# A two-layer hybrid block on one core: six convolution groups whose accumulators lie in PSUM alone, a norm without GpSimd, and 64-wide scores with 128 rows in both products

## The chip, the cores and the metric

The kernel runs on one core of a Trainium2 chip. The core has a tensor engine (PE, with its weight load PEld), a vector engine (DVE), a scalar engine (ACT), GpSimd (POOL) and a queue engine that only starts transfers here (SP). The metric is the device time of one execution in microseconds (us), the median of several runs. Before the change it is 2774.14 us, the median of three runs between 2769.54 and 2776.2.

## The reference, cut to what matters

Three blocks follow each other on 512 tokens of width 1024. Block A is a gated causal convolution and a cross-attention to 256 memory rows; block B an attention whose keys are picked by an index score; block C an attention with 64-wide heads beside a gated linear recurrence, then a layer of 16384 experts of which each token takes 16 for each of 8 heads. What the change touches is this:

```python
# block A: 1536 channels, 31 taps, then a norm over the channels, SiLU and a gate
h = a * jax.nn.sigmoid(gl)
h = depthwise_conv(h, conv_w) + conv_b          # each channel with its own 31 weights
y_mix = silu(layer_norm(h, g, b))
y = jnp.concatenate([y_mix, y_mem], axis=-1) * jax.nn.silu(gate)
x = layer_norm(ALPHA * x + y @ w_out, pg, pb)

# block B: index score with 8 heads of width 64, top 128 of up to 512 keys
iscore = relu(einsum('bqhd,bsd->bqhs', q_idx, k_idx))

# block C: grouped attention, 8 query heads and 2 key heads of width 64
s = einsum('bqkgd,bskd->bkgqs', qblk, k) * scale
```

## The kernel before

Activations lie transposed: 128 channels on the partitions, 512 tokens along the row, so the convolution's 1536 channels are 12 tiles `h0` to `h11`. Full precision on PE comes from splitting each operand into a high part (`hi`, `h`) and a rest (`lo`, `l`) and adding three products (`mm3`, L162 to L164). The high part of a weight tile is made on ACT (L156, `whi`), the rest on POOL or DVE (L157, `wlo`), with four buffers each.

A scheduler reads the program, simulates it on a timeline and writes one order for each engine. On the chip each engine runs its list in that order; a row that has to wait holds up all that stand behind it in its list.

Block A (`layer_a`) goes as follows. PE projects the 24 tiles of the convolution's input, then the memory keys and values (`mem_kv`), the memory queries and their attention (`mem_attn`), 16 gate tiles, and the keys and values of block B's memory attention (again `mem_kv`, with the tiles `bk` and `bv`). Beside that, DVE does the convolution: each tap is one instruction over 128x512, `acc = h[t:t+512] * weight + acc` (L599 for the first tap, L601 for the other 30). Tile 2 goes by ACT (product, L587) and POOL (sum, L590), the other eleven by DVE in the groups `CGR`, whose members take turns tap by tap. An accumulator (`cacc`) lies in one of two PSUM banks (tag `cv`); the third member of the one group with three, tile 9, has its accumulator in SBUF (tag `cva`). The last tap writes the result over `h`.

Then the sums over channels come: ACT squares (L259), POOL adds up tiles (L266, L269), PE adds over partitions with a column of ones (L289, tile `cst`), POOL makes the inverse root (L232 to L238), and PE spreads mean and inverse root over all partitions (L837, `Mb`, `Rb`, both in PSUM). In the norm DVE subtracts `Mb` (L606, 12 times); the product with the inverse root is on DVE for tiles 0, 3, 6 and 9 (L613, from PSUM) and on POOL for the other eight (L615, from `Rs`, a copy in SBUF). ACT scales, shifts and takes a tanh (L617, L619), DVE finishes SiLU (L620) and the gate (L622, whose operand comes back from memory by DMA), and the result is split in `yNh` (ACT, L182) and `yNl` (L185; DVE for even, POOL for odd tiles). PE then multiplies by `a_w_out` (tile `out`); it takes the memory part (`y12` to `y15`) first, then `y0` to `y3`, and `y4` to `y11` with a second set of weight tiles.

For 64-wide heads the split lays both parts in one tile: `split64` gives for each of two heads a tile with the high part in one half of the partitions and the rest in the other, and `twin64` gives the key's high part twice and its rest twice, once in each half. `mm64` adds two products, the first over 128 rows (L213), the second over the 64 rows that hold the query's high part (L214). It is called 24 times in block B (tile `isc`, widths 512, 384 and 256) and 32 times in block C (tile `as`, width 512).

Of the kernel before, what the change touches and what calls it, by code (L numbers as in the profile page):

```python
# [16 lines left out]
OP = mybir.AluOpType  # L17
# [28 lines left out]
MLO = 6  # L46
CGR = (0, 1), (3, 4), (5, 6), (7, 8, 9), (10, 11)
NWARM = 8
# [8 lines left out]
class Body:  # L57
# [152 lines left out]
    def mm64(self, ps, q, k, n, start=True, stop=True):  # L210

        r = slice(64 * n, 64 * n + 64)
        self.nc.tensor.matmul(ps, q, k[0], start=start, stop=False)  # L213
        self.nc.tensor.matmul(ps, q[r], k[1][r], start=False, stop=stop)  # L214

# [92 lines left out]
    def run(self):  # L308
        nc = self.nc
# [10 lines left out]
        if True:  # L320
            with self.phase("A", cva=1, slot=12, pcv=4, scr=2, asc=2, app=2, sq=2, accq=1, accs=1, back=4):
                with self.tc.tile_pool(name="mem", bufs=1) as self.mem:
                    self.layer_a()
            if self.stop == "a":
                self.right.close()
                return
            self.banks(mm=(0, 1), s=(2, 5), pt=(3, 4), o=(6, 7))
            with self.phase("B", slot=14, scr=4, asc=2, app=2, logit=3, alibi=2):
                self.layer_b()
# [206 lines left out]
    def layer_a(self):  # L536
        nc = self.nc
# [21 lines left out]
        Y = {}  # L559
        for h in range(4):  # L560
            f = self.scr("qm", tag="back")
            nc.scalar.copy(f, self.proj(W, 24 + h, self.X))
            o = self.mem_attn(self.split(f, f"qm{h}", lo="g"), kv, h)
            f = self.scr("mo")
            nc.scalar.mul(f, o, 0.5)
            nc.sync.dma_start(od[h], f)
        for j in GATES:
            if j == BKV:
                self.bkv = self.mem_kv(self.i["b_w_mkv"], "b", self.bk, "bkv", 8)
            ps = self.proj(W, 28 + j, self.X)  # L570
# [21 lines left out]
        for js in CGR:  # L592
            accs = [self.scr("cacc", tag="cva") if u == 2 else self.bank("cv", "cacc") for u in range(len(js))]
            for t in range(CK):
# [10 lines left out]
        for c in cs:  # L605
            nc.vector.tensor_tensor(c, c, Mb, op=OP.subtract)  # L606
        Rs = self.scr("Rs", tag="accs")
        nc.scalar.copy(Rs, Rb)
        for j in range(12):
            c = cs[j]  # L610
            n = self.scr("cn", tag=("asc", "app")[j % 2])
            if j % 3 == 0:
                nc.vector.tensor_tensor(n, c, Rb, op=OP.mult)  # L613
            else:
                nc.gpsimd.tensor_tensor(n, c, Rs, op=OP.mult)  # L615
            c = n
# [5 lines left out]
            nc.vector.scalar_tensor_tensor(y, c, 0.25, y, op0=OP.mult, op1=OP.mult)  # L622
            Y[4 + j] = self.split(y, f"y{j}", hi="s", lo="vg"[j % 2], x=2 <= j < 10, tag="slot" if j < 2 else "pcv")
        self.new_x()
# [826 lines left out]
```

## Time and profile before

| | before |
|---|---|
| runs | 2774.14 us (2769.54 to 2776.2) |
| profiled execution, device time | 2769.45 us |
| its span, first to last instruction | 2767.6 us |
| PE busy | 2658.0 us (96%) |
| DVE busy | 2138.1 us (77%) |
| ACT busy | 1235.6 us (45%) |
| POOL busy | 973.6 us (35%) |
| mean granted clock of PE | 0.981 |

The times below count from the start of the span. "Busy" is the time in which an engine had an instruction in work. Matmuls are pipelined: one of 128x512 is shown with 0.39 us, yet the next starts 0.23 us later, so for PE the distance from start to start tells what one costs. The granted clock is a share of 2.4 GHz; there are two levels, 2.4 and 1.2 GHz, and a number between them is a mean over a stretch.

### The profile page before, as it was taken

Reading aid. Unit: us, or ns where it says so; the run is one execution under the profiler, and the core shown is the slowest. Engines: PE = TensorE matmul, PEld = TensorE weight load, DVE = VectorE, ACT = ScalarE, POOL = GpSimd, SP = SyncE. Lnnn points to the kernel's source line nnn. Section 1 sums busy time; section 2 is a strip of 40 time slices with the busy share of each in tenths; the row PEclk is TensorE's granted clock in tenths of the full one; section 3 lists DMA queues with packets and bytes.
Section 4 is the critical chain, followed back from the end, with each engine's and each line's share of the span. In section 5 each row is a group of like instructions: output and inputs, shape, how many; then the busy total and the mean of one; then the engine's idle time right before and its main releaser. Section 6 shows DMA issues by size and latency. Waiting matters only on the chain.

```text
span 2767.6 us, 39611 instructions
## 1 busy us (share of the span) xinstructions
PE 2658.0 (96%) x14197; PEld 2316.9 (84%) x14197; DVE 2138.1 (77%) x4185; ACT 1235.6 (45%) x2155; POOL 973.6 (35%) x702
## 2 busy tenths in 40 slices
PE   9989999999999999999999898999999999999998
PEld 7878879688889877778899897999977888888887
DVE  8999875685566767754679999999677777887855
ACT  4536555455545344443424354546433333433433
POOL 5956654223224745454341522221111111211101
PEclk9999999999999999999999999999999999999999
DMA  5233455232255211136534667688988998999853
GB/s 180 92 107 118 134 170 166 61 100 81 88 184 182 92 57 51 57 107 195 174 98 138 223 224 267 233 300 309 367 305 306 323 320 308 336 353 338 317 166 99
DMA packets 205014, 534.71 MB, mean 193 GB/s; under 512 B 17681, under 2 KB 100497, under 8 KB 186897
## 3 DMA queue, kind: packets, MB, share of 16 engines
q1 hardware_dynamic: 176544, 387.83, 42.5%
q0 software_dynamic: 18432, 134.23, 12.9%
q10 hardware_dynamic: 9840, 10.12, 1.2%
q8 instruction: 112, 1.84, 0.3%
q14 instruction: 86, 0.70, 0.1%
HBM read 465.26 MB, written 66.85 MB: 192 GB/s over the span
## 4 chain that ended last, share of the span: by engine, by line
PE 50%; DVE 13%; DMA 9%; issue 4%; ACT 2%; POOL 1%; SPq 0%; DVEq 0%; POOLq 0%; ACTq 0%
PE mm L163 9%; PE mm L164 9%; PE mm L162 9%; DMA grow<-peer_uv,pidx 4%; PE po L162 3%; DMA vraw<-peer_uv 3%; PE po L163 3%; PE po L164 3%; DMA as<-a_spill 3%; DVE wlo L157 2%; DVE oh L1177 2%; PE out L162 2%; PE out L163 1%; PE out L164 1%; PE gp L1181 1%
## 5 line engine op out<-in xcount | busy, mean ns | idle before, releaser
L156 ACT CAST whi<-wraw 128x1024 fp32r<-128x1024 f32 x360 | 377.3, 1049 | 460.5 <-PE mm L163 242.6
L157 POOL TENSOR_TENSOR wlo<-wraw,whi 128x1024 fp32r<-128x1024 f32 x157 | 380.6, 2427 | 428.7 <-ACT whi L156 382.7
L1206 POOL DMA_INDIRECT grow<-peer_uv,pidx x128 | 173.8, 1358 | 748.6 <-DVE pacc L1216 711.2
L157 DVE TENSOR_TENSOR wlo<-wraw,whi 128x1024 fp32r<-128x1024 f32 x203 | 271.8, 1346 | 58.9 <-ACT whi L156 52.6
L163 PE MATMUL po<-vlo,wh 128*128 128x512 f32 x768 | 302.4, 394 | 0.3 <-DVE vlo L157 0.2
L164 PE MATMUL po<-vhi,wl 128*128 128x512 f32 x768 | 300.4, 393 | 0.0
L601 DVE SCALAR_TENSOR_TENSOR cacc<-h,vecs,cacc 128x512 f32<-128x512 f32 x319 | 235.0, 799 | 0.4
L162 PE MATMUL po<-vhi,wh 128*128 128x512 f32 x768 | 210.4, 399 | 18.4 <-ACT vhi L156 18.4
L1209 DVE SCALAR_TENSOR_TENSOR grow<-grow,hrow 128x1024 f32<-128x1024 f32 x128 | 159.0, 1242 | 54.6 <-DMA grow<-peer_uv,pidx 54.5
L157 DVE TENSOR_TENSOR vlo<-vraw,vhi 128x1024 fp32r<-128x1024 f32 x128 | 156.4, 1222 | 43.5 <-ACT vhi L156 43.2
L162 PEld LDWEIGHTS po<-vhi,wh 128*128 128x128 f32 x768 | 143.7, 189 | 47.7 <-ACT vhi L156 22.1
L1216 DVE SCALAR_TENSOR_TENSOR pacc<-grow,pwc,pacc 128x1024 f32<-128x1024 f32 x127 | 168.3, 1325 | 8.4 <-ACT pwc L1212 7.2
L163 PEld LDWEIGHTS po<-vlo,wh 128*128 128x128 f32 x768 | 144.9, 189 | 32.9 <-DVE vlo L157 2.3
L156 ACT CAST vhi<-vraw 128x1024 fp32r<-128x1024 f32 x128 | 133.8, 1046 | 82.7 <-DMA vraw<-peer_uv 78.7
L164 PEld LDWEIGHTS po<-vhi,wl 128*128 128x128 f32 x768 | 145.0, 189 | 29.4
L1211 ACT ACTIVATE pwc<-pac 128x1 f32<-128x1 f32 x128 | 26.1, 204 | 258.5 <-DVE grow L1209 258.3
L1182 ACT COPY stage<-gp 128x512 f32<-128x512 f32 x96 | 103.4, 1096 | 53.8 <-PE gp L1181 53.5
L162 PE MATMUL mm<-X0h,whi 128*128 128x512 f32 (+2 forms) x294 | 108.6, 374 | 13.9 <-ACT pa L1198 13.0
L164 PE MATMUL mm<-X0h,wlo 128*128 128x512 f32 (+2 forms) x294 | 107.2, 365 | 9.7 <-DVE wlo L157 9.6
L1181 PE MATMUL gp<-oh,oh 128*128 128x128 f32 x768 | 104.3, 282 | 11.2 <-DVE oh L1177 11.0
L1177 DVE TENSOR_SCALAR oh<-iota,rTs 128x128 f32<-128x128 f32 x384 | 113.8, 363 | 0.0
L1181 PEld LDWEIGHTS gp<-oh,oh 128*128 128x128 f32 x768 | 99.5, 194 | 15.4 <-issue 8.2
(975 smaller groups left out, 7828.2 us busy)
## 6 DMA issues: line engine op xcount, KB each, us to landing
wraw<-peer_uT SPq DMA_DIRECT2D x128, 512.0 KB, 5.7
vraw<-peer_uv SPq DMA_DIRECT2D x128, 512.0 KB, 6.5
gates<-stage SPq DMA_DIRECT2D x12, 2048.0 KB, 7.8
G<-gates SPq DMA_DIRECT2D x32, 768.0 KB, 9.5
wraw<-a_w_in SPq DMA_DIRECT2D x43, 512.0 KB, 3.6
wraw<-c_w_in SPq DMA_DIRECT2D x42, 512.0 KB, 3.6
wraw<-b_w_in SPq DMA_DIRECT2D x39, 512.0 KB, 3.5
a_spill<-pa SPq DMA_DIRECT2D x84, 192.0 KB, 4.5
```

The costliest lines, as they stand in the source:

```text
L156: nc.scalar.copy(h, src)
L157: (nc.gpsimd if lo == "g" else nc.vector).tensor_tensor(l, src, h, op=OP.subtract)
L162: nc.tensor.matmul(ps, w[0], x[0], start=start, stop=False)
L163: nc.tensor.matmul(ps, w[0], x[1], start=False, stop=False)
L164: nc.tensor.matmul(ps, w[1], x[0], start=False, stop=stop)
L601: nc.vector.scalar_tensor_tensor(a if t < CK - 1 else cs[j], src, wc, a, op0=OP.mult, op1=OP.add)
L1177: nc.vector.tensor_scalar(oh1[:, u], rows, tr[:, 0, t0 + u:t0 + u + 1], tr[:, 2, t0 + u:t0 + u + 1], op0=OP.is_equal, op1=OP.mult)
L1181: nc.tensor.matmul(ps[:, u * 128:(u + 1) * 128], oh2[:, u], oh1[:, u], start=True, stop=True)
L1182: nc.scalar.copy(stage[:, :, q4 * 4:q4 * 4 + 4].rearrange("p n t -> p t n"), ps.rearrange("p (t n) -> p t n", t=4))
L1206: nc.gpsimd.indirect_dma_start(out=gt, out_offset=None, in_=self.i["peer_uv"], in_offset=bass.IndirectOffsetOnAxis(ap=self.idx[:, n:n + 1] ...
L1209: nc.vector.scalar_tensor_tensor(gt[:, :D], gt[:, :D], 1.0, self.hrow, op0=OP.mult, op1=OP.mult, accum_out=ac)
L1216: nc.vector.scalar_tensor_tensor(self.acc, gt[:, D:], wc, self.acc, op0=OP.mult, op1=OP.add)
```

## The change

The two groups (7, 8, 9) and (10, 11) become (7, 8), (9, 10) and (11,). All accumulators of the groups take the two PSUM banks, and the SBUF buffer `cva` is gone. In the norm all twelve products with the inverse root are on DVE from PSUM, so POOL's eight and ACT's copy `Rs` go, and all twelve `yNl` are on DVE, six of them from POOL. In `mm64` the second product takes all 128 rows of query and key like the first, so that it also adds the product of both rests.

```diff
-CGR = (0, 1), (3, 4), (5, 6), (7, 8, 9), (10, 11)
+CGR = (0, 1), (3, 4), (5, 6), (7, 8), (9, 10), (11,)
...
     def mm64(self, ps, q, k, n, start=True, stop=True):
-        r = slice(64 * n, 64 * n + 64)
         self.nc.tensor.matmul(ps, q, k[0], start=start, stop=False)
-        self.nc.tensor.matmul(ps, q[r], k[1][r], start=False, stop=stop)
+        self.nc.tensor.matmul(ps, q, k[1], start=False, stop=stop)
...
-            with self.phase("A", cva=1, slot=12, pcv=4, scr=2, asc=2, app=2, sq=2, accq=1, accs=1, back=4):
+            with self.phase("A", slot=12, pcv=4, scr=2, asc=2, app=2, sq=2, accq=1, accs=1, back=4):
...
-            accs = [self.scr("cacc", tag="cva") if u == 2 else self.bank("cv", "cacc") for u in range(len(js))]
+            accs = [self.bank("cv", "cacc") for _ in js]
...
-        Rs = self.scr("Rs", tag="accs")
-        nc.scalar.copy(Rs, Rb)
...
-            if j % 3 == 0:
-                nc.vector.tensor_tensor(n, c, Rb, op=OP.mult)
-            else:
-                nc.gpsimd.tensor_tensor(n, c, Rs, op=OP.mult)
+            nc.vector.tensor_tensor(n, c, Rb, op=OP.mult)
...
-            Y[4 + j] = self.split(y, f"y{j}", hi="s", lo="vg"[j % 2], x=2 <= j < 10, tag="slot" if j < 2 else "pcv")
+            Y[4 + j] = self.split(y, f"y{j}", hi="s", lo="v", x=2 <= j < 10, tag="slot" if j < 2 else "pcv")
```

The new lists differ in block A, in a few places of block B and in the expert layer; in the attention of block C the order is the same. Lines after the edited ones have numbers that are smaller by 1, by 6 after the norm.

The first place is DVE's list in the convolution, where tile 6 starts. Before, three accumulators take turns, of which `cacc_3000` (tile 9) is the one in SBUF:

```order
L599 TENSOR_SCALAR cacc_2923<-h6_721,vecs_70 128x512
L601 SCALAR_TENSOR_TENSOR cacc_3000<-h9_922,vecs_70,cacc_3000 128x512
L601 SCALAR_TENSOR_TENSOR cacc_2922<-h5_654,vecs_70,cacc_2922 128x512
L601 SCALAR_TENSOR_TENSOR cacc_2923<-h6_721,vecs_70,cacc_2923 128x512
L601 SCALAR_TENSOR_TENSOR cacc_3000<-h9_922,vecs_70,cacc_3000 128x512
```

With the change, at the same place:

```order
L598 TENSOR_SCALAR cacc_2923<-h6_721,vecs_70 128x512
L600 SCALAR_TENSOR_TENSOR cacc_2922<-h5_654,vecs_70,cacc_2922 128x512
L600 SCALAR_TENSOR_TENSOR cacc_2923<-h6_721,vecs_70,cacc_2923 128x512
L600 SCALAR_TENSOR_TENSOR cacc_2922<-h5_654,vecs_70,cacc_2922 128x512
L600 SCALAR_TENSOR_TENSOR cacc_2923<-h6_721,vecs_70,cacc_2923 128x512
```

The tile with the SBUF accumulator has moved out of the middle to the end, as a member of the pair (9, 10) in PSUM, and tile 11 runs its last 20 taps without a partner, where it ran its last 12 so before.

The second place is POOL's list from the inverse root (`rs_o`) of the convolution's norm on. Before:

```order
L238 TENSOR_TENSOR rs_o<-rs_u,rs_r 128x4
L615 TENSOR_TENSOR cn<-h_280,Rs 128x512
L615 TENSOR_TENSOR cn<-h_347,Rs 128x512
L575 TENSOR_TENSOR g<-th,g 128x512
L578 TENSOR_TENSOR g<-g,ob 128x512
L185 TENSOR_TENSOR y14l<-g,y14h 128x512
L575 TENSOR_TENSOR g<-th,g 128x512
L578 TENSOR_TENSOR g<-g,ob 128x512
L575 TENSOR_TENSOR g<-th,g 128x512
L185 TENSOR_TENSOR y15l<-g,y15h 128x512
L615 TENSOR_TENSOR cn<-h_481,Rs 128x512
L615 TENSOR_TENSOR cn<-h_654,Rs 128x512
```

With the change:

```order
L237 TENSOR_TENSOR rs_o<-rs_u,rs_r 128x4
L574 TENSOR_TENSOR g<-th,g 128x512
L577 TENSOR_TENSOR g<-g,ob 128x512
L185 TENSOR_TENSOR y14l<-g,y14h 128x512
L574 TENSOR_TENSOR g<-th,g 128x512
L577 TENSOR_TENSOR g<-g,ob 128x512
L574 TENSOR_TENSOR g<-th,g 128x512
L185 TENSOR_TENSOR y15l<-g,y15h 128x512
L268 TENSOR_TENSOR accs<-ar_3646,ar_3652 128x512
```

The products `cn` and, further down, the odd `yNl` are gone from POOL; the gate tiles 14, 11 and 15 stay, and next comes work of the output projection.

The third place is PE's list between the convolution's sums (`cst`) and the spread inverse root (`Rb`). Before, from the spread mean (`Mb`) to `Rb`:

```order
L837 MATMUL Mb<-ident,st 128x128 x4
L163 MATMUL mm<-memx_571,whi 128x256
L164 MATMUL mm<-memx_571,wlo 128x256
L162 MATMUL mm<-memx_579,whi 128x256
L163 MATMUL mm<-memx_579,whi 128x256
L164 MATMUL mm<-memx_579,wlo 128x256
L837 MATMUL Rb<-ident,rs_o 128x128 x4
```

With the change:

```order
L831 MATMUL Mb<-ident,st 128x128 x4
L162 MATMUL mm<-X3h,whi 128x512
L163 MATMUL mm<-X3l,whi 128x512
L164 MATMUL mm<-X3h,wlo 128x512
L162 MATMUL mm<-X4h,whi 128x512
L163 MATMUL mm<-X4l,whi 128x512
L831 MATMUL Rb<-ident,rs_o 128x128 x4
```

PE has got further in its own work when it comes to the sums: 13 products of 256 columns that stood behind `cst` stand ahead of it, and it is in the next projection (512 columns) when it comes to `Rb`.

## Rows read from the trace of the kernel before

**Rows 1.** The page's first part: busy time of each engine.
```profile
PE 2658.0 (96%) x14197; PEld 2316.9 (84%) x14197; DVE 2138.1 (77%) x4185; ACT 1235.6 (45%) x2155; POOL 973.6 (35%) x702
```
**Rows 2.** Stretches: length, busy PE, PEld, DVE, ACT, POOL, PE clock, DMA share, GB/s.
```profile
100.00:200.00 100.00, 91.00 (x481) 79.22 (x480) 100.00 (x127) 39.63 (x59) 77.11 (x43) 0.95 0.34 105
```
**Rows 3.** Stretches, instructions of L601 alone: length, DVE busy, PE clock, DMA.
```profile
24.00:127.00 103.00, 86.13 (x128) 1.00 0.32 97
127.00:215.00 88.00, 78.10 (x89) 0.94 0.33 102
```
**Rows 4.** Timeline of DVE: start, duration, engine, line, tiles, count.
```profile
141.48 16.46 DVE L601 SCALAR_TENSOR_TENSOR cacc<-h,vecs,cacc 128x512 f32<-128x512 f32 x15
...
303.47 2.33 DVE L601 SCALAR_TENSOR_TENSOR cacc<-h,vecs,cacc 128x512 f32<-128x512 f32 x3
```
**Rows 5.** PE's waits, 20 to 312 us: total, times, longest.
```profile
PE mm L162 <- ACT mk L413: 5.2, 1, 5.2
PE mvt L422 <- DVE av L222: 2.1, 1, 2.1
PE mvt L422 <- ACT mvT L419: 1.7, 1, 1.7
PE msc L162 <- ACT mp L445: 1.7, 1, 1.7
```
**Rows 6.** Timeline of ACT; in brackets the wait and what ended it.
```profile
160.92 0.37 ACT L413 COPY mk<-mm 128x256 f32<-128x256 f32 x1 [6.66 <-DVE ak L222]
```
**Rows 7.** Stretches as in rows 2, memory keys and values.
```profile
160.00:170.00 10.00, 8.65 (x55) 8.65 (x56) 10.00 (x15) 4.53 (x8) 4.71 (x2) 0.70 0.19 54
...
180.00:190.00 10.00, 10.00 (x40) 8.08 (x40) 10.00 (x16) 3.32 (x6) 2.89 (x2) 0.84 0.25 91
```
**Rows 8.** Timeline of PE where the convolution ends.
```profile
316.64 0.58 PE L289 MATMUL cst<-ones,h 128*128 128x1 f32 x2 [3.51 <-DVE h L601]
```
**Rows 9.** Stretches as in rows 2, convolution's sums.
```profile
310.00:320.00 10.00, 6.49 (x43) 6.28 (x41) 6.85 (x7) 3.54 (x6) 4.71 (x3) 0.81 0.56 204
320.00:330.00 10.00, 10.00 (x62) 9.96 (x62) 2.93 (x7) 1.17 (x3) 3.10 (x9) 0.67 0.22 79
```
**Rows 10.** Groups of instructions, 0 to 700 us: busy, mean ns, idle before.
```profile
L620 DVE SCALAR_TENSOR_TENSOR cn<-th,cn 128x512 f32<-128x512 f32 x12 | 15.0, 1279 | 1.6 <-ACT th L619 1.6
...
L622 DVE SCALAR_TENSOR_TENSOR gb<-cn,gb 128x512 f32<-128x512 f32 x12 | 12.6, 1066 | 3.3 <-DMA gb<-a_gates 3.2
...
L615 POOL TENSOR_TENSOR cn<-h,Rs 128x512 f32<-128x512 f32 x8 | 10.3, 1291 | 14.7 <-DVE gb L622 6.6 <-issue 4.4 <-ACT Rs L608 3.7
```
**Rows 11.** Timeline of DVE, the subtraction of the mean.
```profile
328.09 7.27 DVE L606 TENSOR_TENSOR h<-h,Mb 128x512 f32<-128x512 f32 x12 [3.07 <-PE Mb L837]
```
**Rows 12.** Stretches as in rows 2, output projection of block A.
```profile
360.00:370.00 10.00, 8.86 (x39) 6.82 (x37) 9.91 (x12) 7.90 (x13) 5.97 (x5) 1.00 0.46 130
370.00:380.00 10.00, 5.27 (x11) 3.25 (x12) 9.97 (x10) 8.03 (x12) 5.53 (x4) 0.54 0.29 68
```
**Rows 13.** Timeline of PE where the second set of weights begins.
```profile
371.15 0.80 PE L162 MATMUL out<-y4h,whi 128*128 128x512 f32 x1 [2.29 <-ACT whi L156]
```
**Rows 14.** Timeline of PE, products of the 64-wide scores.
```profile
493.10 0.40 PE L213 MATMUL isc<-kih,qi 128*128 128x512 f32 x1
493.34 0.40 PE L163 MATMUL mm<-X1l,whi 128*128 128x512 f32 x1
...
972.14 0.49 PE L214 MATMUL as<-k0l,rq 64*128 64x512 f32 x1
972.57 0.50 PE L213 MATMUL as<-k0h,rq 128*128 128x512 f32 x1
973.00 0.49 PE L214 MATMUL as<-k0l,rq 64*128 64x512 f32 x1
```
**Rows 15.** Stretches as in rows 2, both places of the 64-wide scores.
```profile
490.00:545.00 55.00, 52.95 (x196) 36.26 (x195) 36.89 (x71) 20.59 (x37) 13.86 (x7) 0.94 0.19 58
960.00:1240.00 280.00, 266.87 (x1376) 208.21 (x1375) 200.45 (x389) 114.32 (x219) 142.74 (x132) 1.00 0.21 66
```
**Rows 16.** PE's waits, 1260 to 2768 us, the largest.
```profile
PE po L162 <- ACT vhi L156: 18.4, 10, 3.4
```

## The prediction

> **What bounds the kernel now.** I read the page first: PE is busy for 96% of the span, DVE for 77% [rows 1]. A gain therefore has to show on PE, as less work or as less waiting, and a part of the change that only frees DVE or POOL is worth what PE stood still for. The stretches then say where that is. In block A's middle DVE has not a moment's rest, 100.00 of 100 us, while PE has gaps, 91.00 of 100 [rows 2]: there DVE sets the pace. PE's list of waits names them: one of 5.2 us for a copy on ACT, and three of 2.1, 1.7 and 1.7 us, 10.7 us together [rows 5]. ACT's timeline shows that the copy of the long one had itself stood for 6.66 us behind a split on DVE [rows 6]. Where the convolution ends PE waits again, 3.51 us for the last tap [rows 8], and in the output projection it stands for the second set of weights [rows 13]. The two places of the 64-wide scores look different: PE is busy for 52.95 of 55 and 266.87 of 280 us [rows 15], so there the work of PE counts itself, and waiting is 2 and 13 us.
>
> **The convolution.** Eleven tiles of 31 taps, 341 instructions, are the same before and after. What changes is how long one takes. Between 24 and 127 us, with both accumulators in PSUM, 128 of them keep DVE for 86.13 us, 0.673 each; between 127 and 215 us, while tile 9 with its accumulator in SBUF takes turns with the others, 89 keep it for 78.10, or 0.878 [rows 3]. The worst piece is 15 in 16.46 us [rows 4]. POOL is at work for 77% of this time [rows 2], and what differs is that tile 9's taps read two operands from SBUF. The difference is 89 x 0.205 = 18.2 us of DVE, and I expect all of it to go.
>
> The Trainium skill says the same of two-operand work (SBUF — State Buffer, Who interferes with whom): a DVE instruction with two inputs in SBUF contends with a GpSimd instruction that reads SBUF, one with at most one such input does not. The trace agrees with 0.878 against 0.673 us.
>
> For PE this is worth the waits that came from a late DVE: up to 10.7 us, and the slower clock behind them. The granted clock is 0.70 and 0.84 of 2.4 GHz in two stretches of 10 us behind the waits [rows 7], a mix with the 1.2 GHz level that costs 10 x 0.30 + 10 x 0.16 = 4.6 us. That makes 15.3 at most. The 15 taps ahead of the first split took 16.46 us [rows 4] and would take 10.1 at the undisturbed pace, so DVE gets there over 6 us earlier and the longest wait should go whole; one of the short ones may stay. I take **13**, between 5 (the longest wait alone) and 15.3.
>
> **The end of the convolution.** PE gains 13, DVE 18.2 us, so the last tap comes some 5 us earlier as PE sees it. Against that, tile 11 runs 20 taps alone instead of 12, and alone a tap follows the last after 2.33 / 3 = 0.78 us [rows 4] instead of 0.67, so 8 x 0.11 = 0.9 us are lost. PE also has 13 products of 256 columns more in front of its sums. The wait of 3.51 us [rows 8] should vanish but for some tenths; it cannot turn into much more than that, because rows of DVE in front of the last taps (the splits of `bk` and two `wlo`) wait for PE themselves. What is left is the clock: 0.81 and 0.67 in the two stretches around the sums [rows 9], 1.9 + 3.3 = 5.2 us. If the wait made PE slow, it goes too; if the sums themselves do it, 24 products of one column, it stays. I take half of it and the wait: **6**, between 0 and 8.7. The third group adds no wait of its own: the accumulator of tile 11 takes the bank of tile 9, whose last reader stands ahead on the same engine.
>
> **The norm.** DVE gets 8 products and 6 rests more, 14 instructions. Undisturbed, twelve subtractions take 7.27 us, 0.606 each [rows 11], so that is 8.5 us. POOL's eight products, 1.29 us each, go, and with them the disturbance that they and the six rests cause: SiLU and gate take 1.279 and 1.066 us in the mean for the same shape [rows 10], 12 x 0.67 + 12 x 0.46 = 13.6 us above the undisturbed pace. I take a third of that to come from POOL's gate tiles, which stay, so some 9 us come back: DVE comes out even. The chain gets shorter, since POOL waited 6.6 us for DVE in five places [rows 10], and those are hops that no longer exist. On PE, the output projection lost 1.14 + 4.73 us of idle time and, at 0.54, 4.6 us of clock [rows 12], 10.5 in all, to weights that ACT could only cast after it had done `y6h` [rows 13]. In the new lists all four casts stand behind `y6h` again, and PE arrives with three us more of its work done. So most of this stall stays: I take **3**, between -8.5 (the 14 instructions uncovered) and 10.5.
>
> **The 64-wide scores.** A product of 128 rows and 512 columns lets the next one start 0.24 us later (493.10 to 493.34). Into and out of one with 64 rows it is 0.43 us on either side (972.14, 972.57, 973.00) [rows 14]. PE's weight load does not run ahead across that border. With all rows in both products there is no border: 2 x 0.20 = 0.40 us for each of the 32 in block C, 12.8 us; in block B some of the 24 are narrower and one side is less, which I put at 0.35, 8.4 us. That is 21.2 us of PE, at places where PE is busy for 95 to 96% [rows 15]. Not all of it arrives: between the products stand softmax and index sums, and DVE is at 72% in block C. A quarter lost to such waits leaves **16**, between 4 and 21.2.
>
> Here a rule of the Trainium skill speaks against the edit (TensorEngine Tiling (Array Packing), Key Properties): tiles that take half of the rows work independently and can run in parallel, so giving them up could cost. The same list says that a change of tiling mode drains the engine, which is what the 0.43 us look like; the 64-row products here stand alone between 128-row ones, and nothing runs beside them. By the first rule alone this term would be zero or a loss, by the second it is the 21 us.
>
> **Sum.** 13 + 6 + 3 + 16 = 38 us from the profiled execution's 2769.45 us: 2731 us. That execution is the lowest of those shown, 4.7 us under their median, and a median of the changed kernel may lie that much higher, so I predict **2732**.
>
> **Rivals.**
> Time that comes back as waiting. DVE is already full in block A, and in blocks B and C what PE saves it could stand idle for the next softmax. For it speaks that short waits are there already, 13 us in block C [rows 15]; against it, that they are much smaller than PE's work. It gives half of each large term and little of the small ones, 8 + 2 + 0 + 8 = 18: 2751 us.
> The border isn't what costs. If 0.43 us belong to these products for another reason than the row count, `mm64` does not do what it is meant to and its term is 0: 38 - 16 = 22, 2747 us. Against it stands that the same first product (L213) has a successor after 0.24 us where that is a 128-row one.
> Slower than before. The expert layer's lists have moved too, though its code hasn't. There PE waits 18.4 us in ten places, up to 3.4 us each, for casts that wait for the expert's rows from memory [rows 16]. If a transfer comes late in the new order, each such wait is 3.4 us; from eleven more on, all 38 us are gone, and with fifteen the time is 2782 us. Nothing says that the new order is worse there, and the ten of before may as well get fewer.
>
> **How the numbers follow.** The forecast has 0.66, with a range of its own from 2715 to 2745; the returned waiting 0.18; the border 0.11; slower through the expert layer 0.04; 0.01 is left. The range from 2714 to 2755 takes in the forecast and both middle cases but not the last, and its low end is where nearly all bounds are reached (15 + 9 + 8 + 21 = 53 would be 2716). Differences under 0.3%, 8.3 us, cannot be told from none in this kernel. Faster by more than that is 0.93 (the three cases that gain, less what a weaker sum leaves), the same 0.04, slower 0.03.
>
> **What will show it.** Right: taps at 0.67 to 0.69 us from 127 to 215 us; no wait of PE for `mk` near 156 us; `cst` reached without a wait of 3.5 us and some 15 us earlier; SiLU and gate near 0.7 us where POOL is still; products of L212 and L213 0.23 us apart. Wrong: the same idle time of PE at other rows of block A, PE standing longer before `y4`, or in block C a PE that is busy for far less than 95% while the stage is as long as before.

## The result and the profile after

| | before | after |
|---|---|---|
| runs | 2775.17 us (2769.54 to 2785.57, 4 runs) | 2736.78 us (2735.62 to 2744.85, 4 runs) |
| ratio, 95% interval | | 0.9877 (0.9857 to 0.9897) |
| profiled execution | 2769.45 us | 2735.62 us |
| mean granted clock of PE | 0.981 | 0.984 |

The change makes the kernel 38 us faster in the medians (29 to 40 by the interval) and 34 us between the two profiled executions; 2732 was forecast. The page's first part, against [rows 1]:

```profile
PE 2635.2 (96%) x14197; PEld 2315.2 (85%) x14197; DVE 2115.8 (77%) x4199; ACT 1233.8 (45%) x2154; POOL 951.0 (35%) x688
```

PE has the same 14197 products and is busy for 22.8 us less, so two thirds of those 34 us are PE's own pace (borders, clock), and one third is waiting that went. DVE has 14 instructions more and is busy for 22.3 us less.

**The convolution.** The stretch of [rows 2], and the taps alone in stretches like those of [rows 3] (they stand in L600 now; columns as there):

```profile
100.00:200.00 100.00, 100.00 (x544) 87.02 (x543) 98.45 (x152) 45.92 (x76) 83.06 (x47) 1.00 0.39 118
...
24.00:127.00 103.00, 84.66 (x126) 0.98 0.31 96
127.00:200.00 73.00, 61.14 (x92) 1.00 0.40 121
```

DVE is nearly as full as before, but it does 152 instructions in these 100 us, where it did 127; a tap takes 61.14 / 92 = 0.665 us where it took 0.878 in the mean. PE has no gap left and runs at 1.00. Its waits from 20 to 312 us, all of them, against [rows 5]:

```profile
PE memT L398 <- ACT memf L401: 3.6, 1, 3.6
PE cst L288 <- DVE h L600: 0.7, 1, 0.7
PE mm L164 <- POOL wlo L157: 0.5, 1, 0.5
```

The waits for `mk`, `mvt` and `msc` are gone. (The first row belongs to the transposes of the memory rows, from 64 to 86 us; before, it was 1.6 us, and in a second trace of the changed kernel it is 1.6 us again.)

**Where the convolution ends.** PE's timeline, against [rows 8], and the stretches around it, against [rows 9]:

```profile
303.03 0.38 PE L288 MATMUL cst<-ones,h 128*128 128x1 f32 x2 [0.71 <-DVE h L600]
...
304.89 3.55 PE L288 MATMUL cst<-ones,sq 128*128 128x1 f32 x16
```

```profile
300.00:310.00 10.00, 9.29 (x58) 9.08 (x57) 4.22 (x8) 2.48 (x5) 4.77 (x6) 0.72 0.50 154
310.00:320.00 10.00, 10.00 (x56) 8.80 (x55) 6.95 (x11) 3.05 (x5) 1.46 (x5) 0.94 0.26 79
```

PE arrives at 302.3 instead of 313.1 us and waits 0.71 instead of 3.51. The clock still falls here.

**The norm and the output projection.** Groups of instructions from 303 to 400 us (columns as in [rows 10]), and the stretches in which `y4` comes, against [rows 12]:

```profile
L614 DVE SCALAR_TENSOR_TENSOR cn<-th,cn 128x512 f32<-128x512 f32 x12 | 9.5, 798 | 1.1 <-ACT th L613 1.1
L616 DVE SCALAR_TENSOR_TENSOR gb<-cn,gb 128x512 f32<-128x512 f32 x12 | 8.2, 688 | 6.6 <-DMA gb<-a_gates 6.5
```

```profile
350.00:360.00 10.00, 8.81 (x36) 6.19 (x35) 10.00 (x14) 8.50 (x12) 0.00 (x0) 1.00 0.54 164
360.00:370.00 10.00, 10.00 (x46) 8.23 (x45) 6.31 (x11) 2.40 (x4) 0.00 (x0) 1.00 0.64 188
```

SiLU and gate take 0.80 and 0.69 us each where they took 1.28 and 1.07. POOL is idle for 20 us, PE loses 1.2 us of them, and the clock stays at 1.00; before, PE lost 5.9 us in such 20 and the clock was at 0.54 in one half. One wait on DVE is longer, 6.5 us for the gate's operand from memory against 3.2 [rows 10]; PE waits 1.1 us in all in the output projection, for weights.

**The 64-wide scores.** PE's timeline, against [rows 14]:

```profile
945.76 0.50 PE L212 MATMUL as<-k0h,rq 128*128 128x512 f32 x1 [0.52 <-DVE rq L195]
946.10 0.40 PE L213 MATMUL as<-k0l,rq 128*128 128x512 f32 x1
946.34 0.39 PE L212 MATMUL as<-k0h,rq 128*128 128x512 f32 x1
946.57 0.40 PE L213 MATMUL as<-k0l,rq 128*128 128x512 f32 x1
946.80 1.05 PE L886 MATMUL hl<-hQ,kc 128*128 128x128 f32 x8
```

Two calls take 946.80 - 945.76 = 1.04 us. The steps are 0.23 us, but the first one behind a wait is 0.34. The rows of the weight load (PEld) show what the border does: before, the weights of a product were loaded only when that product itself started (first row, of the kernel before); now they are loaded when its predecessor starts (second row, the weights of the product of 946.34).

```profile
972.57 0.19 PEld L213 LDWEIGHTS as<-k0h,rq 128*128 128x128 f32 x1 [0.24 <-issue]
```

```profile
946.10 0.19 PEld L212 LDWEIGHTS as<-k0h,rq 128*128 128x128 f32 x1
```

The whole stage of block C's scores, from the first to the last, has the same 1292 products in the same order before and after. Here it is before, after, and in the second trace of the changed kernel (columns as in [rows 2]):

```profile
971.71:1234.20 262.49, 249.85 (x1292) 194.30 (x1292) 187.12 (x368) 105.94 (x205) 132.48 (x124) 1.00 0.21 65
```

```profile
945.76:1198.80 253.04, 239.51 (x1292) 195.40 (x1293) 186.60 (x368) 105.69 (x205) 133.29 (x124) 1.00 0.22 67
```

```profile
941.60:1197.80 256.20, 243.28 (x1291) 198.75 (x1292) 186.80 (x368) 105.73 (x205) 133.41 (x124) 0.98 0.21 66
```

PE has 10.3 us less work, and 9.5 of them arrive; its idle time grows from 12.6 to 13.5 us. The second trace is 3.2 us longer because the granted clock fell there (0.98 over the stage); neither trace of the kernel before has that.

**The account by stages.** Starts read from the traces, in us. Each of the two kernels has two traces; the second ones are from the last experiments.

| start of | before | after | gain so far |
|---|---|---|---|
| first sum of the convolution's last tile | 316.6, 314.6 | 303.0, 301.7 | 13.3 |
| first score of block B (`isc`) | 493.1, 492.0 | 470.9, 468.4 | 22.9 |
| last score of block B | 542.4, 541.4 | 515.9, 511.9 | 28.0 |
| first score of block C (`as`) | 971.7, 970.6 | 945.8, 941.6 | 27.5 |
| last score of block C | 1234.2, 1233.1 | 1198.8, 1197.8 | 35.4 |
| first product of the expert layer (`po`) | 1971.3, 1971.8 | 1937.2, 1935.9 | 35.0 |
| end of the span | 2767.6, 2768.9 | 2733.8, 2729.9 | 36.4 |

The gain is made in block A and at the two places of the scores; between them and behind them the stages are as long as before, within 1.4 us in the mean.

### The profile page after: what moved, and what is told of

It reads as the page before. It is cut to its first block, busy times and chain, and to the rows that moved or that the text cites. A ratio compares the mean times of both kernels' runs of the same rounds, so it can differ in the third digit from the quotient of the medians.

```text
span 2733.8 us, 39603 instructions
## 1 busy us (share of the span) xinstructions
PE 2635.2 (96%) x14197; PEld 2315.2 (85%) x14197; DVE 2115.8 (77%) x4199; ACT 1233.8 (45%) x2154; POOL 951.0 (35%) x688
## 4 chain that ended last, share of the span: by engine, by line
PE 51%; DVE 15%; DMA 10%; issue 5%; ACT 2%; POOL 1%; SPq 0%; DVEq 0%; POOLq 0%; ACTq 0%
PE mm L162 9%; PE mm L164 9%; PE mm L163 9%; DMA grow<-peer_uv,pidx 6%; PE po L163 3%; PE po L164 3%; PE po L162 3%; DMA vraw<-peer_uv 3%; DVE wlo L157 2%; DVE oh L1171 2%; PE out L162 2%; PE out L163 2%; PE out L164 2%; PE gp L1175 1%; DVE pacc L1210 1%
## 5 line engine op out<-in xcount | busy, mean ns | idle before, releaser
L600 DVE SCALAR_TENSOR_TENSOR cacc<-h,vecs,cacc 128x512 f32<-128x512 f32 x319 | 218.0, 749 | 0.6
L1175 PEld LDWEIGHTS gp<-oh,oh 128*128 128x128 f32 x768 | 98.8, 193 | 17.2 <-issue 8.8
```

The source lines that it names most:

```text
L600: nc.vector.scalar_tensor_tensor(a if t < CK - 1 else cs[j], src, wc, a, op0=OP.mult, op1=OP.add)
L1175: nc.tensor.matmul(ps[:, u * 128:(u + 1) * 128], oh2[:, u], oh1[:, u], start=True, stop=True)
```

## The experiments

The first four put parts of the change alone, or all but one. Each ratio is against runs of the kernel before that were timed beside it (medians of 2775.24, 2775.0 and 2769.44 us).

**The convolution alone** (before, with the new groups, both kinds of accumulator in PSUM).

```diff
-CGR = (0, 1), (3, 4), (5, 6), (7, 8, 9), (10, 11)
+CGR = (0, 1), (3, 4), (5, 6), (7, 8), (9, 10), (11,)
...
-            accs = [self.scr("cacc", tag="cva") if u == 2 else self.bank("cv", "cacc") for u in range(len(js))]
+            accs = [self.bank("cv", "cacc") for _ in js]
```

> The kernel before with the six groups and all accumulators in PSUM, nothing else. Theory (tile 9's SBUF accumulator was slowed by GpSimd, and a late DVE made PE wait): taps fall to 0.67-0.69 us each everywhere, PE's waits for the memory keys go, PE reaches the convolution's sums 12 us earlier, and the time falls by 12 to 16 us, to about 2760. Rival (DVE had slack, the gain comes from the norm): DVE is early, but PE waits the same time for the norm's results, and the time falls by less than 5 us.

Measured: 2756.83 us (6 runs), ratio 0.9934 (0.9913 to 0.9956), so 12 to 24 us faster. The first sum of the last tile comes at 299.7 us, 16 us earlier, and block B's scores begin at 473.1, 19 us earlier. It is the largest part of the change.

**The norm alone** (before, with the products on DVE and no POOL in the splits).

```diff
-        Rs = self.scr("Rs", tag="accs")
-        nc.scalar.copy(Rs, Rb)
...
-            if j % 3 == 0:
-                nc.vector.tensor_tensor(n, c, Rb, op=OP.mult)
-            else:
-                nc.gpsimd.tensor_tensor(n, c, Rs, op=OP.mult)
+            nc.vector.tensor_tensor(n, c, Rb, op=OP.mult)
...
-            Y[4 + j] = self.split(y, f"y{j}", hi="s", lo="vg"[j % 2], ...
+            Y[4 + j] = self.split(y, f"y{j}", hi="s", lo="v", ...
```

> The kernel before with the norm's twelve products and twelve rests on DVE alone, nothing else. Theory (DVE comes out even, the hops through GpSimd go): the stall of PE ahead of y4 shrinks from 10 us to some 5, time down by 3 to 9 us, about 2768. Rival (14 more instructions on the busiest engine): time up by 3 to 8 us, about 2780.

Measured: 2782.54 us (12 runs), ratio 1.0021 (1.0006 to 1.0036), 2 to 10 us slower. My theory missed this, and the rival's size came, but not at the rival's place. That place got faster: from the first sum to block B's scores it is 170.8 us, before 176.5 and 177.4. PE's waits in the output projection, from 325 to 395 us, first in this kernel, then with the convolution alone, which has the old norm:

```profile
PE out L164 <- DVE wlo L157: 0.9, 1, 0.9
PE out L162 <- ACT whi L156: 0.8, 2, 0.5
```

```profile
PE out L164 <- DVE wlo L157: 3.9, 1, 3.9
PE out L162 <- ACT whi L156: 3.3, 1, 3.3
```

The time is lost elsewhere, and the record shows only where: the first product of the expert layer still starts level with before (1972.6 us against 1971.3 and 1971.8); from there to the end this trace takes 811.6 us where before takes 796.3 and 797.1, in code that is the same. PE's largest wait there, against [rows 16]:

```profile
PE po L162 <- ACT vhi L156: 26.5, 9, 6.3
```

**The scores alone** (before, with 128 rows in both products).

```diff
-        r = slice(64 * n, 64 * n + 64)
...
-        self.nc.tensor.matmul(ps, q[r], k[1][r], start=False, stop=stop)
+        self.nc.tensor.matmul(ps, q, k[1], start=False, stop=stop)
```

> The kernel before with 128 rows in both products of the 64-wide scores, nothing else. Theory (each 64-row product holds up the weight load on both its sides): 0.23 us from start to start in place of 0.43, time down by 13 to 16 us, about 2760, of it 9 to 10 in block C and 4 in block B. Rival (the attention waits for softmax anyway): the products are closer together but PE's waits grow by as much, time down by less than 5 us.

Measured: 2762.23 us (8 runs), ratio 0.9949 (0.9926 to 0.9972), 8 to 21 us faster. Block B's scores take 44.9 us (before 49.3 and 49.4), block C's 253.1 (before 262.5 twice): 13.9 us in the two stages, split as expected.

**The norm put back** (the changed kernel with the norm as before; the diff is that of the norm alone, backwards).

> The changed kernel with the norm as it was before (eight products and six rests on GpSimd, the copy on ACT). Theory (the norm is worth 3 to 9 us on its own, beside the others): 2740 to 2746 us, and SiLU and gate instructions go back from 0.80 and 0.69 to over 1.0 us. Rival (the norm only helps where the convolution is late): within 2 us of the changed kernel, 2737.

Measured: 2742.41 us (2733.86 to 2745.68, 4 runs), ratio 0.9887 (0.9867 to 0.9908). That is the changed kernel's time, within what the runs differ. Block B's scores begin at 474.4 us, 3.5 and 6.0 later than in the two traces of the changed kernel, but block C's begin at 945.7, where those have 945.8 and 941.6, and they end at 1198.2 against 1198.8 and 1197.8. So the norm's gain is real at its place and gone before block C's scores are done. What takes it is the clock: from block B's last score to block C's first, this kernel needs 426.5 us, the changed kernel 429.8 and 429.7, and there the clock falls in both of its traces (0.66 and 0.67 from 840 to 855 us), here it does not. The stretch in this kernel and in the changed one (columns as in [rows 2]):

```profile
840.00:855.00 15.00, 13.14 (x88) 11.64 (x87) 13.96 (x16) 8.95 (x22) 11.77 (x9) 1.00 0.53 166
```

```profile
840.00:855.00 15.00, 13.79 (x62) 11.73 (x60) 11.31 (x15) 6.77 (x16) 8.54 (x7) 0.66 0.42 138
```

In block C the changed kernel's second trace loses another 3.2 us to the clock (above). Why the clock falls in one kernel and not in the other is open.

**One accumulator in SBUF** (the changed kernel, six groups, tile 10 accumulating in SBUF).

```diff
...
-            accs = [self.bank("cv", "cacc") for _ in js]
+            accs = [self.scr("cacc", tag="cva") if j == 10 else self.bank("cv", "cacc") for j in js]
```

> The changed kernel with one thing put back: tile 10 of the convolution, in its group of two with tile 9, accumulates in SBUF; the six groups and all else stay. My theory (a tap that reads two operands from SBUF is disturbed by GpSimd): the 62 taps of this group take 0.85 to 0.90 us in the mean instead of 0.69, so DVE is 10 to 18 us later at the end of the convolution, the first sum of the last tile comes at 311 to 318 us instead of 303.0, and the median is 2745 to 2755 us instead of 2736.8. Rival (the new grouping in pairs, not the memory, made the taps faster): the taps stay at 0.67 to 0.70 us, the first sum of the last tile stays within 3 us of 303, and the median within 5 us of 2737.

Measured: 2744.86 us (4 runs), ratio 0.9881 (0.9843 to 0.9919); the first sum of the last tile at 315.0 us instead of 303.0 and 301.7. As it needs no bank, the scheduler lets tile 10 run beside tiles 5 to 8 and ends it at 226 us. The page's row of all taps but each tile's first and last and, in DVE's timeline, the last tap of tile 10; then the same row of the changed kernel:

```profile
L600 DVE SCALAR_TENSOR_TENSOR cacc<-h,vecs,cacc 128x512 f32<-128x512 f32 x319 | 235.2, 800 | 0.4
...
226.12 2.22 DVE L600 SCALAR_TENSOR_TENSOR h<-h,vecs,cacc 128x512 f32<-128x512 f32 x1
```

```profile
L600 DVE SCALAR_TENSOR_TENSOR cacc<-h,vecs,cacc 128x512 f32<-128x512 f32 x319 | 218.0, 749 | 0.6
```

The same 319 taps cost 17.2 us more, with one accumulator moved and the groups kept. The memory of the accumulator is the cause, not the number of groups; the time, 8 us above the changed kernel's median, lies just below what was expected, and its interval holds the changed kernel's ratio, so the time by itself shows nothing.

**The 64-row product twice** (the changed kernel, with the low part counted twice).

```diff
+        r = slice(64 * n, 64 * n + 64)
...
-        self.nc.tensor.matmul(ps, q, k[1], start=False, stop=stop)
+        self.nc.tensor.matmul(ps, q[r], k[1][r], start=False, stop=False)
+        self.nc.tensor.matmul(ps, q[r], k[1][r], start=False, stop=stop)
```

> The changed kernel, but the second product of the 64-wide scores has 64 rows again and is issued twice, one right behind the other, so that the computation counts the low part twice. My theory (0.20 us is the price of each border between 64 and 128 rows, not of a 64-row product): the two 64-row products follow each other after 0.23 to 0.25 us, the steps into the first and out of the second are 0.43 us, and each of the 32 calls in the index scores over 128 rows is 0.60 to 0.65 us longer; the stage from the first to the last of these products is 16 to 20 us longer than the 253 us of the changed kernel. Rival (a 64-row product itself needs 0.43 us): the step between the two 64-row products is 0.43 us too, a call is 0.80 to 0.85 us longer, and the stage 24 to 28 us.

("Index scores" there means block C's `as`.) Measured: 2769.95 us (10 runs), ratio 0.9991 (0.9971 to 1.0012). PE's timeline at the same place:

```profile
948.08 0.50 PE L213 MATMUL as<-k0h,rq 128*128 128x512 f32 x1 [0.50 <-DVE rq L195]
948.51 0.50 PE L214 MATMUL as<-k0l,rq 64*128 64x512 f32 x1
948.85 0.39 PE L215 MATMUL as<-k0l,rq 64*128 64x512 f32 x1
949.17 0.50 PE L213 MATMUL as<-k0h,rq 128*128 128x512 f32 x1
```

The steps are 0.43, 0.34 and 0.32 us (0.44, 0.33, 0.33 in the next call): neither theory's list. Their sum, 1.09, is what the border theory gives: a call of before is 0.43 + 0.43 = 0.86 [rows 14], and a second 64-row product adds 0.23 to it, the price of an ordinary product, not 0.43. Block C's scores take 1221.3 - 948.1 = 273.2 us, 17 and 20 more than the changed kernel (256.2 and 253.0), where 16 to 20 was expected against the rival's 24 to 28. But this stage does not hold the same work: it has 1313 products, 11 fewer than the 1292 of the changed kernel with 32 added, and 6.8 us of it are at the low clock. So it is the steps that decide, not the stage.

**One product only** (the changed kernel, where `mm64` leaves out its second product).

```diff
-        self.nc.tensor.matmul(ps, q, k[0], start=start, stop=False)
-        self.nc.tensor.matmul(ps, q, k[1], start=False, stop=stop)
+        self.nc.tensor.matmul(ps, q, k[0], start=start, stop=stop)
```

> The changed kernel without the second product of the 64-wide scores (the part with the low halves of the keys is left out). It takes 56 x 0.23 = 12.9 us of work from PE at most, in the two places where the change saved PE its borders. My theory (there PE's work sets the time, and about three quarters of what it saves arrives): 8 to 12 us less, median 2725 to 2729. Rival (what PE saves here is lost to waits for the maxima and the softmax, and the gain of the changed kernel was already at its limit): less than 4 us, median 2733 to 2737, with longer waits of PE for ACT and DVE in the same two places.

Measured: 2748.59 us (4 runs), ratio 0.9895 (0.9863 to 0.9927): nothing gained, so the theory fell; the rival's median was missed too, by 12 us. Block B's scores take 43.1 us by their starts (45.0 and 43.5 with both products), block C's 256.0 (253.0 and 256.2). PE's largest wait from 935 to 1225 us, here and in the changed kernel:

```profile
PE as L212 <- ACT ap L996: 9.2, 10, 2.4
```

```profile
PE as L212 <- ACT ap L997: 3.8, 9, 0.9
```

The wait is for the exponential of the softmax. In block C's scores PE's idle time grows from 13.5 to 19.8 us, 6.3 of the 7.4 us that 32 products cost (32 x 0.23), so most of what PE saves beyond the borders is lost to waits (and the clock is 0.99 over the stage, where the changed kernel's first trace has 1.00). The kernel as a whole is even slower, by its expert layer: 823.8 us there, 796.6 and 794.0 in the changed kernel. (That trace is of the slowest of its four runs, 8 us above their median.)

**Fewer sums** (the changed kernel, with 8 of the 16 one-column products at the convolution's end).

```diff
                     srcs = [s0] + [p[part] for p in self.last[tt // 2]]
+                    srcs = srcs[-1:] if self.name == "cst" else srcs
```

> The changed kernel, but the sums of the convolution's norm take only the last of their three sources: 8 products of one column instead of 24, and the statistics leave out the rest. The granted clock around these sums was 0.72 and 0.94 in the changed kernel although PE's wait ahead of them had shrunk to 0.7 us. Theory (the one-column sums themselves slow the clock): in the 20 us from the first of them the clock stays at 0.95 or above, and the output projection starts 5 to 8 us earlier (16 sums of 0.25 to 0.35 us, and 3 us of clock). Rival (the clock falls for what lies ahead of the sums or for the waits that follow): the clock still drops to about 0.7 in one stretch of 10 us, and the output projection starts 3 to 5 us earlier, the time of the products alone.

(The sums have two sources, not three: the trace of the changed kernel shows 32 instructions for them, two for each product, and this one 16. So 8 of 16 products are left, not 8 of 24.) Measured: 2743.2 us (4 runs), ratio 0.9877 (0.9845 to 0.9909). PE alone in stretches of 2 us, here and then in the second trace of the changed kernel (length, busy PE, clock, DMA share, GB/s):

```profile
300.00:302.00 2.00, 2.00 (x16) 0.79 0.43 160
302.00:304.00 2.00, 2.00 (x10) 0.50 0.01 2
304.00:306.00 2.00, 2.00 (x7) 0.50 0.56 205
306.00:308.00 2.00, 2.00 (x6) 0.50 0.40 125
```

```profile
302.00:304.00 2.00, 2.00 (x19) 0.92 0.36 133
304.00:306.00 2.00, 2.00 (x11) 0.50 0.01 2
306.00:308.00 2.00, 2.00 (x11) 0.50 0.64 229
308.00:310.00 2.00, 2.00 (x10) 0.50 0.09 33
310.00:312.00 2.00, 2.00 (x10) 0.88 0.00 0
```

Half of the sums gone, and the clock costs the same: 2 x (0.21 + 3 x 0.50) = 3.4 us here, 2 x (0.08 + 3 x 0.50 + 0.12) = 3.4 there. The rival was right that it falls all the same, and the output projection starts 5.1 and 3.8 us earlier than in the two traces of the changed kernel, of which 1.9 lie behind the first sum (24.6 us from it to the projection, against 26.5); the rest lies ahead of it and is not the edit's.

**Wider work between the sums** (the changed kernel, with a product of 128 columns behind each finished sum).

```diff
+                        if self.name == "cst" and n > 0:
+                            nc.tensor.matmul(ps[:, 128:256], src[:, tt * 128:(tt + 1) * 128], b.ones, start=True, stop=True)
```

> The changed kernel with eight products of 128 columns added, whose results nobody reads: one behind each finished sum of the convolution's norm, into free columns of the same bank. The short wait of 0.7 us ahead of the sums stays. Theory (a run of one-column products lets the clock fall to 1.2 GHz; with wider work in between it stays): the granted clock is above 0.95 in every 2 us from the first sum on, and the 3 us that it cost come back less some 1.5 us for the added products, so the output projection starts 1 to 2 us earlier after the first sum of the last tile than the 26.5 us of the changed kernel. Rival (the clock falls for the gap ahead of the sums, whatever follows): it is 0.50 for some 7 us again, and the projection starts 2 to 4 us later, the added products at the low clock.

Measured: 2741.33 us (4 runs), ratio 0.9883 (0.986 to 0.9907). The same view:

```profile
302.00:304.00 2.00, 2.00 (x20) 1.00 0.02 8
304.00:306.00 2.00, 2.00 (x14) 0.70 0.54 184
306.00:308.00 2.00, 2.00 (x11) 0.50 0.20 78
308.00:310.00 2.00, 2.00 (x11) 0.94 0.00 0
```

Both missed. With the same wait of 0.7 us ahead, the clock falls later and costs 2 x (0.30 + 0.50 + 0.06) = 1.7 us, half; the added products eat that, and the projection starts 26.7 us after the first sum of the last tile, 26.5 in the changed kernel. So neither the wait alone nor the one-column products alone decide; how they share it is open.

**More banks for block B's scores** (the changed kernel, `isc` in four banks instead of two).

```diff
-                ps = self.bank("s", "isc")
+                ps = self.bank(("s", "o")[h // 2 % 2], "isc")
```

> The changed kernel, but the scores of the sparse attention (24 pairs of 64-wide products) alternate between the two PSUM banks of this stage and the two that stand beside them instead of keeping to two. My theory (in this stage part of what PE saved became waits for the ReLU on ACT that frees a bank): the waits for it, 3.4 us in five places, fall below 1 us, the stage from the first to the last of these products is 2 to 4 us shorter than 45.0, and the median is 0 to 4 us lower than the changed kernel's. Rival (the waits are for ACT's and DVE's work itself, not for a bank): the waits move to other rows, the stage stays within 1 us of 45, and the median within 5 us.

Measured: 2740.5 us (4 runs), ratio 0.9883 (0.9861 to 0.9905). The scores are done in 31.9 us, but the wait is still 3.4 us in total, and block C's scores begin at 941.8 us, as in the second trace of the changed kernel (941.6): the scheduler only moved other work behind them. No gain, for neither of the reasons given.

**Both kernels again**, without an edit, for a second trace of each.

> The kernel before, once more, for a second trace. Theory (the order of instructions is fixed and what differs between executions are the transfers of the expert layer): up to the first sum of the expert products every milestone is within 1 us of the first trace (493.1, 971.7 and 1971.3 us), and what differs in the time, up to 15 us, lies behind 1971 us. Rival (executions differ everywhere): the milestones ahead of it move by several us.

> The changed kernel once more, for a second trace. Theory: its milestones up to the first expert product are within 1 us of the first trace (303.0, 470.9, 945.8, 1198.8 and 1937.2 us), so that the gain of 34 us there is the change's, and only the expert layer differs. Rival: they move by several us, and the differences of 2 to 4 us that were read between single traces mean nothing.

Measured: 2770.7 and 2731.72 us (one run each). The starts are in the account above. Before repeats within 2.0 us in every row; after differs by 1.0 to 4.2 us (945.8 and 941.6). So the theory nearly holds for before (1.1, 1.1 and 0.5 us at its three milestones) and is too narrow for after: a difference under some 4 us between single traces says nothing, and the account uses means of two. The expert layer repeats too: 796.3 and 797.1 us before, 796.6 and 794.0 after. The kernels of the experiments that have an edit take 795.7 to 823.8 us there. PE stands idle for 22 to 25 us of that stage in the traces in which it takes 794 to 797 us, and for 29 to 42 us in the others. The code of that stage is the same in all of them; the scheduler writes another order for each. That the order is the cause was not tried by itself, and one trace of each is little: the runs of the kernel before lie between 2768.3 and 2785.6 us, and both of its traces are of runs near the lower end.

## Why the prediction was right

The forecast case came, 5 us above its number by the median of four runs. By its terms, with means of two traces:

| term | predicted | measured | how |
|---|---|---|---|
| convolution | 13 | 12.2 | PE arrives 10.5 us earlier, with 15 products (13 of 256 columns, two of 128; about 1.7 us) more done by then |
| end of the convolution | 6 | 4.5 | wait 3.5 to 0.7; clock 5.1 to 3.4 |
| norm, output projection | 3 | 6.2 | from the sums to block B's scores 9.65, less 1.7 of products moved ahead and 1.7 of clock |
| 64-wide scores | 16 | 13.0 | 5.1 in block B, 7.9 in block C, where the second trace loses 3.2 to the clock |
| elsewhere | 0 | 0.5 | up to the expert layer -0.9, in it 1.4 |
| sum | 38 | 36.4 | spans, 2768.25 to 2731.85 |

That the sum is closer than its terms is luck: the norm gave 3 us more than its term and the scores 3 less.

**Convolution.** Right, and for the stated reason: taps at 0.665 us, no wait of PE for `mk`, and one accumulator put back into SBUF takes 12.6 of the 13.3 us at the first sum away again. The sentence of the Trainium skill (SBUF — State Buffer, Who interferes with whom) on two operands in SBUF agrees with this: a tap of tile 10 beside GpSimd is shown with 2.22 us, an undisturbed one with 0.75. The 0.878 us of the prediction are a mean, though: no tap takes that long (see the last point of the document).

**End of the convolution.** The wait went as forecast, to tenths of a microsecond. The clock was mis-sized: I gave back half of 5.2 us for a wait that vanishes, but the wait vanished and 3.4 of 5.1 us stayed. The sums are 16 products and not the 24 that I counted. The low clock costs the same with half of them, and half with wider work in between.

**Norm.** The size was off, 3 against 6. The step that failed: "In the new lists all four casts stand behind `y6h` again [...] So most of this stall stays". They do stand behind it, but `y6h` starts 35.5 us after DVE's first subtraction (314.3 to 349.8 us) instead of 41.4 (328.1 to 369.5), and PE's waits here fall from 5.9 us [rows 12] to 1.1. I had let DVE "come out even" with 9 us back from SiLU and gate; these gave 9.9. (The 13.6 us behind that set durations against the distance from start to start, 0.606 us; against the duration of a subtraction, 0.68, they are 11.8.) Not counted were DVE's splits, which POOL's work disturbs too: before, `y0l` and `y2l` took 1.03 and 1.20 us, now 0.69 and 0.68. That is 0.9 us; in the trace with the convolution alone, so with the old norm, four of them take 1.04 to 1.75 us. The rest of the 5.9 us by which `y6h` comes earlier I put down to the hops through POOL, which I had named without a price; no run takes that apart. The 10.5 us that I set as the bound were too high, since 4.6 of them are clock over a stretch of 10 us in which PE stood still for 4.73. And some of the clock only moved: it is 1.00 in the output projection now, but 0.66 and 0.77 from 430 to 445 us in the two traces (0.94 in the 30 us that correspond before, 440 to 470).

At the kernel's end, though, the norm is worth nothing that the runs can tell: putting it back leaves the time the same, and alone it made the kernel 6 us slower, by the trace through a slower expert layer. For the sum as a whole, 3 was no worse than 6.

**Scores.** Right in kind. The border is the price (the 64-row product itself costs 0.23 us, as any), two calls fall from 4 x 0.43 = 1.72 to 1.04 us with the same number of products. The size was off in the price, not in the share that is lost. The price is 0.34 us a call instead of 0.40, since a first step behind a wait still takes 0.34. In the first trace PE's work falls by 10.3 us in block C, where I had counted 12.8, and by 7.6 in block B (47.64 to 40.05 us busy, two other products fewer), where I had 8.4. Of these 17.9 us, 9.5 and 4.3 arrive, 13.8, close to the 13.9 of the edit alone; 4.2 became waiting, the quarter that I had taken off. But it is not spread evenly: in block C waits took 0.9 us, in block B 3.3 of 7.6 (there the wait for the ReLU rose from 1.7 to 3.4 us, and one of 1.4 us for a split on DVE came up). The 13.0 of the table are lower because of the clock in the second trace. Removing the second product altogether gains nothing more: behind the borders the softmax is the limit. So the first rival has the right mechanism, but it took half and the runs show a quarter.

**The other rivals.** "The border isn't what costs" is refuted by the 0.23 us. The one that ended slower had the right place: the expert layer's time differs by 28 us between these kernels, though not by the 51 that I had priced. In the changed kernel it didn't come, and that is luck too: in their traces, eight of the ten edited kernels take 807 to 824 us there against 794 to 797. In the norm alone it turned a gain at its place into a loss. For a program whose order is written anew with each edit, 0.04 was a low chance.

The rule weighed against the edit, that tiles of half the rows can run in parallel (the Trainium skill, TensorEngine Tiling (Array Packing), Key Properties), had no hold here: there was nothing beside the 64-row products.

## What to carry to other kernels

Read what one instruction costs by neighbours: a tap at 0.67 us or 0.88 in the mean, a product at 0.23 or 0.43 us, is the same work, and the difference is the gain, before any instruction is removed. Divide such a gain by place, and look at the idle time of the engine there before and after: of PE's work saved, nine tenths arrived in block C and less than three fifths in block B, and a second cut at the same places brought nothing. Compare the granted clock of a stage before you call a difference waiting. Where a scheduler writes the order anew, compare by stages and not by the end, and take two traces before believing 4 us.

## What the runs showed of the hardware

- The border is one of rows, not of columns. In block C products with a tile of 128 rows and 64 columns (`ao`, 128*64) alternate with full ones every 0.12 us, with no longer step at either side; a single product of 64 rows among such of 128 (512 columns) costs some 0.20 us on each side. PE's timeline of the changed kernel:

```profile
966.61 0.28 PE L1009 MATMUL ao<-apt,V 128*64 128x256 f32 x1
966.73 0.28 PE L1008 MATMUL ao<-apt,V 128*128 128x256 f32 x1
966.85 0.28 PE L1009 MATMUL ao<-apt,V 128*64 128x256 f32 x1
```

- The low clock at the sums costs 3.4 us after a wait of 0.7 us, with 16 one-column products or with 8, and 1.7 us with eight products of 128 columns between them; a wait of 0.91 us for `y4`'s weights between products of 512 columns left it at 1.00 (350 to 360 us above).
- A tap with both operands in SBUF is not slow as such; it waits for POOL. In the kernel before, 17 instructions of L601 take over 1 us (1.12 to 2.93), all between 132 and 217 us. Each of them starts while POOL has an instruction with two operands in SBUF in work, and ends 0.54 to 0.56 us after that one; with tile 10 put back into SBUF, 16 do the same. The last of them and what POOL did then, in the kernel before (213.60 + 2.81 = 216.41, 213.47 + 2.39 = 215.86):

```profile
213.60 2.81 DVE L601 SCALAR_TENSOR_TENSOR h<-h,vecs,cacc 128x512 f32<-128x512 f32 x1
```

```profile
213.47 2.39 POOL L157 TENSOR_TENSOR wlo<-wraw,whi 128x1024 fp32r<-128x1024 f32 x1
```
